# One recurrence head's projections and one more gate computed in the dense stage, read back from DRAM, and the first dense unit opened earlier

## The chip, the cores and the metric

The kernel runs on one core of a Trainium2 chip. The metric is the device time of the whole program in microseconds, the median of three runs. The engines have the names of the profile: PE (TensorE, matmuls and transposes), DVE (VectorE), ACT (ScalarE), POOL (GpSimd) and SP (SyncE, which here only issues DMAs). Each engine works off a list of instructions of its own in a fixed order.

## What is computed

One block of a streaming encoder over 1024 tokens of width 1024, in float32:

```python
h = rmsnorm(x, norm_mix_g)
z = h @ w_in          # hq hf hi hg | fq fk fv ff | mq | gate_logits
y_a = hgrn2(hq, hf, hi, hg)      # 4 heads, state 128 x 128
y_b = fox(fq, fk, fv, ff)        # 8 heads of 64, causal, forgetting
y_c = memory_attention(mq, mem)  # 4 heads of 128 over 256 tokens
gates = sigmoid(gate_logits).reshape(B, T, 3, 1024)
merged = gates[0]*(y_a @ w_br_hgrn) + gates[1]*(y_b @ w_br_fox) + gates[2]*(y_c @ w_br_mem)
x = x + merged @ w_out
x = x + conv_glu_ffn(rmsnorm(x, norm_ffn_g))
```

For a recurrence (HGRN2) head, three of the projections go through a nonlinearity before the scan: q by silu, the forget logit by a sigmoid, whose logarithm is summed along the chunk, and the output gate by silu. The fourth, hi, gives the values.

## The kernel before

Each float32 product is done as three matmuls on operands split into a high and a low part (`mm3`, L160 to L162: high x high, low x high, high x low). A split is a cast on ACT (L166) and a subtraction on DVE (L174); the weights' parts are wh and wl, the normed input's uh and ul. A projection goes in chunks of 128 output columns, each in two halves of 512 tokens. `cm_chunk` takes a half in 8 steps of 128 rows, 24 matmuls of 512 columns; a half sits in one of three PSUM banks (pp) until it is evacuated.

The stages, in the program's order:

1. First two gates, the memory's keys and values (`mem_values`, `mem_keys`), and a gate that covers what lies between (`first_cover`, `cover`). `SEQ` writes down the order of these steps. `differences` makes the families T1 to T4, sums and differences of blocks of the input, with their splits.
2. The dense stage. `dense_unit` takes two chunks at once by a Strassen-Winograd scheme: seven products in place of eight, each 4 x 3 matmuls, on sums of weight blocks (s1 to s4) that DVE adds and that are split like weights. `PAIRS` lists the chunks: the memory's queries (12 to 15), then gates. `put` adds what a product has to be added to, applies tanh to a gate and writes it to DRAM (`gd`; the queries to `mqd`).
3. The forgetting attention, four pairs of heads (`fox_attn(p, i)`), in which transposes, casts, softmax and the products po alternate between the engines. So that PE does not wait for them, matmuls that depend on nothing are woven in (`weave`): the next pair's projections, plain gate chunks (`gates_early`, their count in `NFOX`) and, in the last pair, the recurrence's values (`hgrn_values`, evacuated by ACT into Vf at L1001; Vf's place is also read by the split of the last attention values, vhl). Before the attention is over, the static order already holds the recurrence's first projections.
4. The recurrence. `open_hgrn` loads the masks (hmf, cast to hm at L989) and rs. `hgrn_prep(h)` computes a head's three projections: evacuation with the token's scale on DVE into gt or zt (L1032), tanh on ACT (L1034), then a clip and scale on POOL (ha, L1037) or a product on DVE (hq, hz, L1040). `hgrn_mix(h)` takes the head's logarithm (Ln, L1065), scans it (L1071), and does for each half a stack of levels with exponentials (Xk, X, L1081 to L1117), products pl (L1088), kE and its transposes (L1151 to L1160), states and po. Mix h is woven with the projections of head h + 1; head 0's run before the first mix.
5. Branches, output projection, and the feed-forward part.

[...] Where no other order is given, a scheduler sets each engine's list when the program is built; `ahead(..., AHEAD)` gives the woven attention and mixes priority, and `tc.issue_after` keeps an instruction behind a named other one. Buffers rotate within a tag (`bufs=`): the three gate tiles (gt) and the three banks pp matter here. `spread_dma` copies the norm's row to SBUF (L353) and sends it through DRAM to all partitions (rx), by which all gates are scaled.

Of the kernel before, what the change touches and what calls it, by code (L numbers as in the profile page):

```python
# [14 lines left out]
P = 128  # L15
# [76 lines left out]
def run_all(gen):  # L92
    for _ in gen:
        pass
# [15 lines left out]
def tile_block(ctx: ExitStack, tc: tile.TileContext, xT, memT, x_rows, mem_rows, vec, fbias, mats, hmask, w_first, w_cm, w_hi, w_fqk, w_fv,  # L110
# [20 lines left out]
    def ps_tr():  # L131
        return pz.tile([P, HB], F32, tag="tr", name="tr", bufs=2)
# [217 lines left out]
    def spread_dma(r, rcol, row, name, ps):  # L350

        PE.transpose(ps[:8, :P], rcol, ident)
        S.copy(row, ps[:8, :P])  # L353
# [50 lines left out]
    def mem_keys():  # L404
        mkt = keys[0]
        for hh in range(2):
            ptr = ps_tr()
            for h in range(2):
                for m in range(2):
                    PE.transpose(ptr[:, (2 * h + m) * P:(2 * h + m + 1) * P],  # L410
                                 mkt[:, m, (2 * hh + h) * P:(2 * hh + h + 1) * P], ident)
            S.activation(mkf[:, 2 * hh:2 * hh + 2, :], ptr.rearrange("p (h m) -> p h m", h=2), AF.Copy, scale=mgk)
        G.dma_start(kvd[:, 0, :], mkf.rearrange("p a b -> p (a b)"))
# [36 lines left out]

    gd = tc.dram_tile([len(order), 2, P, HB], F32, name="gd")
    mqd = tc.dram_tile([4, P, T], F32, name="mqd")

    home = {"pool": p0}

# [49 lines left out]
    def differences():  # L505

        b = [[xk[k + 4 * c][:, n * HB:(n + 1) * HB] for c in range(2) for n in range(2)] for k in range(4)]
        new_family(pt, "T1", 2)
        for t in range(4, 8):
            with tc.issue_after(late["keys"].ins), tc.issue_after(late["square"].ins):  # L510
                S.activation(xk[t], xk[t], AF.Copy, scale=col(C_GX + t))
        for k, (b11, b12, b21, b22) in enumerate(b):
            with tc.issue_after(late["x_low"].ins):
                V.tensor_sub(b11, b11, b12)
            h, l = (t[k] for t in fam["T1"])
            with tc.issue_after(late["square"].ins):
                S.activation(h, b11, AF.Copy, scale=col(C_GX + k))
            V.scalar_tensor_tensor(out=l, in0=b11, scalar=col(C_GX + k), in1=h.bitcast(F32), op0=ALU.mult, op1=ALU.subtract)
        yield
        new_family(pt, "T2", 2)  # L520
        for k, (t1, b12, b21, b22) in enumerate(b):
            with tc.issue_after(late["x mean"].ins):
                V.scalar_tensor_tensor(out=t1, in0=t1, scalar=ngx[:, k:k + 1], in1=b22, op0=ALU.mult, op1=ALU.subtract)
            family_block("T2", k, t1)
        yield
        new_family(pt, "T3")
        for k, (t2, b12, b21, b22) in enumerate(b):
            with tc.issue_after(late["x mean"].ins):
# [12 lines left out]

    gen = {}

    def families_step():
        if "differences" not in gen:
            gen["differences"] = differences()
        next(gen["differences"])

    named = dict(f1=families_step, f2=families_step, f3=families_step, mn=mem_norm, me=keys_out, mk=mem_keys, mv=mem_values, xn=x_norm, lk=load_late, lx=lambda: load_rows(*T2[2:], *T1[2:]), ly=lambda: load_rows(*T2[:2]), lz=lambda: load_rows(*T2[2:]), ev=first_gates, cv=first_cover)
    for what in SEQ:  # L550
        if what in named:
            named[what]()
        else:
            steps[what[0]](int(what[1]))
    p0.release()

    ps1 = Rounded(tc, name="ps1", bufs=1, side="right", reuse_waits="tile")
    def block(b, k):
        if b in fam:
            return [t[k] for t in fam[b]]  # L560
# [10 lines left out]
    class Dense:  # L571
# [1 line left out]
        half = None  # L573

        def snap(self, ps):
            e = ps1.tile([P, HB], F32, tag="fe", name="fe", bufs=3)
# [6 lines left out]
        def sum_of(self, i, a, b):  # L583
            t = ps1.tile([P, HB], F32, tag=f"s{i}", name=f"s{i}")
            V.tensor_add(t, a, b)
            return t

        def operand(self, src):
# [6 lines left out]
            split(S, h, l, src)  # L595
            return h, l

    dense = Dense()

    def dense_unit(src, put, first, families):  # L600

        raw = []
        whole = None if first else dense.raw()
        for i in range(2):
            if first:
                t = wp.tile([P, 4 * 264], F32, tag="raw", name="raw", bufs=2)[:, :2 * HB]
                t = t.rearrange("p (a b) -> p a b", a=2)
            else:
                t = whole[:, 2 * i:2 * i + 2, :]
            G.dma_start(t, src[:, 2 * i:2 * i + 2, :])  # L610
            raw += [t[:, 0, :], t[:, 1, :]]
        a11, a21, a22, a12 = raw
        x, y = ps_proj(), ps_lg()
        o1 = dense.operand(a11)
        if first:
            o6 = dense.operand(a12)
        s1 = dense.sum_of(1, a21, a22)
        o2 = dense.operand(s1)
        s2 = dense.sum_of(2, s1, a11)
# [12 lines left out]
        s4 = dense.sum_of(4, s2, a12)  # L632
        product(y, dense.operand(s4), "B22", False)
        put(0, 1, y, e2)
        s3 = dense.sum_of(3, a11, a21)
        product(x, dense.operand(s3), "T3", False)
        put(1, 1, x, e5)
        if not first:
            z = ps_tr()
            product(z, dense.operand(a12), "B21", True)  # L640
            put(0, 0, z, e1)
        product(x, dense.operand(a22), "T4", False)
        put(1, 0, x, None)

    def dense_put(chunks):

        def put(c, n, ps, e):
            ch = chunks[c]
            sl = slice(n * HB, (n + 1) * HB)
            t = gate_tile()  # L650
            if ch < 16:
# [357 lines left out]
    def held(gen, lag):  # L1009

        while True:
# [5 lines left out]
                    return  # L1017
            yield

    def hgrn_prep(h):  # L1020
        ph = state["ph"]
        qt = ph.tile([P, T], F32, tag="hq", name=f"hq_{h}", bufs=2)
        at = ph.tile([P, T], F32, tag="ha", name=f"ha_{h}", bufs=2)
        for what, base, dst in ((0, 4, at), (1, 0, qt), (2, 8, None)):
# [3 lines left out]
            for n, ps in cm_chunk(w_cm[base + h], KC, uh, ul, h == 3 and what == 2):  # L1028
                sl = slice(n * HB, (n + 1) * HB)

                zt = ph.tile([P, HB], F32, tag="zt", name="zt") if h else gate_tile()
                V.tensor_mul(zt, ps, rx[:, sl])  # L1032
                d = dst[:, sl]
                S.activation(d, zt, AF.Tanh, scale=0.5)  # L1034
# [766 lines left out]
```

## Time and profile before

| | |
|---|---|
| median of three runs | 1702.52 us (1702.37 to 1704.14) |
| profiled execution, its own time | 1703.12 us |
| its span, first to last instruction | 1701.3 us |
| granted TensorE clock | 1.000 |
| busy: PE, DVE, ACT, POOL | 99%, 68%, 47%, 19% |
| opening of the dense stage | about 69 to 86 us |
| last po of the attention | 682.6 us |
| first transposes of kE in the recurrence | 700.3 us |

In the rows of a timeline stand the start, the duration, the engine, the line, the operation, the tiles written and read, and in brackets the idle time before it with what ended it. A row of waits has the total, the number and the longest. A row of windows has the stretch, then the busy time and count of PE, of its weight loads, DVE, ACT and POOL, the granted clock, the DMAs' share and GB/s. Matmuls overlap, so the duration of one is not its cost; the distance of two starts is. The profiled execution is 0.6 us above the median of the runs.

### The profile page before, as it was taken

The page shows a single profiled execution, that of the slowest core. Times are in us where ns is not written, and L with a number is a line of the kernel's source. Part 1 is how long each engine was busy: PE and PEld are TensorE (multiplying, and loading weights), DVE is VectorE, ACT ScalarE, POOL GpSimd, SP SyncE. Part 2 cuts the span into 40 slices and gives each one's busy share as a digit, 9 for nine tenths or more (in the row PEclk, how much of TensorE's full clock was granted, in tenths as well). Part 3 has the DMA queues.
Part 4 walks back from the last instruction along what each step waited for, and adds up shares of the span by engine and source line. Part 5 has one row for each costly group of instructions (what it writes and reads, how often), then busy time and mean ns, then how long its engine had stood idle before and what let it go on. Part 6 is the DMA issues. An engine that isn't in the chain of part 4 may idle for free.

```text
span 1701.3 us, 24306 instructions
## 1 busy us (share of the span) xinstructions
PE 1692.3 (99%) x8965; PEld 1452.3 (85%) x8965; DVE 1151.9 (68%) x2057; ACT 801.5 (47%) x1428; POOL 326.7 (19%) x420
## 2 busy tenths in 40 slices
PE   9999999999999999999999999999999999999999
PEld 7788899989898998888888888888888888888887
DVE  6956555665666655786856855987778888775664
ACT  6734455555464553776531334644434444433432
POOL 0200022543433331553310000311111111100000
PEclk9999999999999999999999999999999999999999
DMA  9433242221312111200346552566555444494782
GB/s 369 170 137 114 73 146 76 77 92 45 99 50 87 52 57 57 67 27 18 100 125 216 165 188 99 162 171 172 151 144 141 118 144 147 162 375 142 247 274 87
DMA packets 82774, 227.16 MB, mean 134 GB/s; under 512 B 9680, under 2 KB 12248, under 8 KB 82528
## 3 DMA queue, kind: packets, MB, share of 16 engines
q1 hardware_dynamic: 64464, 160.99, 27.4%
q0 software_dynamic: 18048, 64.50, 13.5%
q8 instruction: 70, 1.15, 0.3%
q14 instruction: 48, 0.39, 0.1%
q10 hardware_dynamic: 144, 0.13, 0.0%
HBM read 180.72 MB, written 67.93 MB: 146 GB/s over the span
## 4 chain that ended last, share of the span: by engine, by line
PE 98%; DVE 1%; DMA 0%; ACT 0%; issue 0%; SPq 0%; DVEq 0%
PE pp L162 21%; PE pp L160 21%; PE pp L161 21%; PE lg L160 4%; PE lg L162 4%; PE lg L161 4%; PE tr L160 3%; PE tr L162 3%; PE tr L161 3%; PE po L951 1%; PE lg L910 1%; PE lg L909 1%; PE po L950 1%; PE po L160 1%; PE po L161 1%; PE po L162 1%
## 5 line engine op out<-in xcount | busy, mean ns | idle before, releaser
L160 PE MATMUL pp<-uh,wh 128*128 128x512 f32 x412 | 163.1, 396 | 0.0
L161 PE MATMUL pp<-ul,wh 128*128 128x512 f32 x412 | 162.9, 395 | 0.0
L162 PE MATMUL pp<-uh,wl 128*128 128x512 f32 x412 | 162.4, 394 | 0.0
L161 PE MATMUL pp<-wl,uh 128*128 128x256 f32 (+1 forms) x512 | 146.2, 286 | 0.0
L162 PE MATMUL pp<-wh,ul 128*128 128x256 f32 (+1 forms) x512 | 146.0, 286 | 0.0
L160 PE MATMUL pp<-wh,uh 128*128 128x256 f32 (+1 forms) x512 | 145.6, 285 | 0.0
L166 ACT CAST wh<-s 128x512 fp32r<-128x512 f32 x113 | 68.2, 620 | 130.8 <-PE pp L161 66.4
L166 ACT CAST wh<-raw 128x1024 fp32r<-128x1024 f32 (+2 forms) x76 | 67.7, 890 | 100.3 <-PE pp L161 88.2
L166 ACT CAST wh<-rw 128x512 fp32r<-128x512 f32 x87 | 53.2, 619 | 107.6 <-PE pp L161 72.0
L160 PEld LDWEIGHTS pp<-wh,uh 128*128 128x128 f32 x512 | 97.3, 190 | 1.2
L161 PEld LDWEIGHTS pp<-wl,uh 128*128 128x128 f32 x512 | 97.4, 190 | 1.0
L162 PEld LDWEIGHTS pp<-wh,ul 128*128 128x128 f32 x512 | 97.4, 190 | 0.9
L1443 POOL DMA_DIRECT2D rw<-in_w_up x44 | 24.1, 555 | 372.8 <-DVE wl L1336 171.8
L166 ACT CAST dwh<-wr 128x1024 fp32r<-128x1024 f32 (+1 forms) x41 | 40.2, 980 | 115.0 <-PE tr L161 40.4
L162 PEld LDWEIGHTS pp<-uh,wl 128*128 128x128 f32 x412 | 77.5, 188 | 15.1
L174 DVE TENSOR_TENSOR wl<-raw,wh 128x1024 fp32r<-128x1024 f32 (+2 forms) x75 | 78.0, 1040 | 18.1 <-ACT wh L166 17.9
L160 PEld LDWEIGHTS pp<-uh,wh 128*128 128x128 f32 x412 | 77.5, 188 | 14.6
L161 PEld LDWEIGHTS pp<-ul,wh 128*128 128x128 f32 x412 | 77.5, 188 | 14.5
L174 DVE TENSOR_TENSOR dwl<-wr,dwh 128x1024 fp32r<-128x1024 f32 (+1 forms) x41 | 46.3, 1130 | 33.6 <-ACT dwh L166 32.5
L925 ACT ACTIVATE pt<-pt,st 128x128 f32<-128x128 f32 (+3 forms) x64 | 49.7, 777 | 40.1 <-DVE st L922 32.0
L927 POOL TENSOR_SCALAR pt<-pt,st 128x128 f32<-128x128 f32 (+3 forms) x64 | 50.7, 793 | 77.5 <-DVE st L926 62.4
L1336 DVE TENSOR_TENSOR wl<-rw,wh 128x512 fp32r<-128x512 f32 x69 | 47.7, 705 | 22.5 <-PE pp L162 18.1
(497 smaller groups left out, 5123.9 us busy)
## 6 DMA issues: line engine op xcount, KB each, us to landing
rw<-in_w_up POOLq DMA_DIRECT2D x44, 512.0 KB, 4.9
sd<-in_w_dn POOLq DMA_DIRECT2D x30, 512.0 KB, 6.2
br<-yd SPq DMA_DIRECT2D x30, 512.0 KB, 5.3
raw<-in_w_cm SPq DMA_DIRECT2D x24, 512.0 KB, 3.4
gd<-gt SPq DMA_DIRECT2D x48, 256.0 KB, 2.0
gt<-gd SPq DMA_DIRECT2D x48, 256.0 KB, 2.7
yd<-fc SPq DMA_DIRECT2D x44, 256.0 KB, 3.0
wr<-sd SPq DMA_DIRECT2D x20, 512.0 KB, 4.6
```

What stands on the lines that cost most here:

```text
L160: PE.matmul(ps, lh, rh, start=first, stop=False, skip_group_check=more)
L161: PE.matmul(ps, lh, rl, start=False, stop=False, skip_group_check=more)
L162: return PE.matmul(ps, ll, rh, start=False, stop=last, skip_group_check=more)
L166: return S.copy(out, in_)
L174: return (sub or V).tensor_sub(l, src, h.bitcast(F32))
L909: PE.matmul(ps[:, :w], qa[i][:, tsl], kh[i][:, s0:s0 + w], start=True, stop=False)
L910: fox_sets[p][3] = PE.matmul(ps[:, :w], qa[i][:, tsl], kl[i][:, s0:s0 + w], start=False, stop=True)
L925: S.activation(pt[:, :ns], pt[:, :ns], AF.Exp, bias=st[:, 2:3], accum_out=st[:, 3:4])
L927: G.tensor_scalar(pt[:, :ns], pt[:, :ns], st[:, 3:4], 0.0, ALU.mult, ALU.add)
L950: PE.matmul(o, vhl[:, sb, :], ph[:, src], start=(sb == 0), stop=False)
L1336: late["split"] = V.tensor_sub(l, src, h.bitcast(F32))
L1443: late["raw"] = G.dma_start(raw[:, 2 * i:2 * i + 2, :], src[:, 2 * i:2 * i + 2, :])
```

## The change

Three projections of recurrence head 0 (chunks 4, 0 and 8) go into the dense stage, and one more gate with them: nine dense units in place of seven. `put` does what `hgrn_prep(0)` did (tanh, clip and scale, or the product) and writes the result to DRAM (`hd`, six writes of 256 KB); `hgrn_load` reads it back in three transfers of 512 KB in place of `run_all(hgrn_prep(0))`. The last pair of the attention loses its gate chunk (`NFOX[6]`). In `SEQ` the first dense unit is opened (`du`: loads, first sums and splits, which use spare places in xk) before the first gates' evacuation and the memory's keys; the casts of T1 and T3 are kept behind the copy of the norm's row on ACT; the keys' transposes use another PSUM bank. Head 1's projections now use the gate tiles.

```diff
-NCOVER, NPAIR = 2, 10
+NCOVER, NPAIR = 2, 11
-NFOX = [0, 3, 0, 3, 0, 3, 1]
+NFOX = [0, 3, 0, 3, 0, 3, 0]
+HEAD0 = {4: 0, 0: 1, 8: 2}
-_dense = [12, 13, 14, 15] + [16 + 8 * br + j for br, j in ORDER[4:4 + NPAIR]]
+_dense = [12, 13, 14, 15] + list(HEAD0) + [16 + 8 * br + j for br, j in ORDER[4:4 + NPAIR]]
...
-       "q0 me k4 q1 k5 c0 ly c1 lz q2 q3 k6 q4 q5 k7 d0 q6 q7 xn d1 mv f1 cv f2 ev mk f3").split()
+       "q0 me k4 q1 k5 c0 ly c1 lz q2 q3 k6 q4 q5 k7 d0 q6 q7 xn d1 mv cv f1 f2 f3 du ev mk").split()
...
-        S.copy(row, ps[:8, :P])
+        late["row"] = S.copy(row, ps[:8, :P])
...
-            ptr = ps_tr()
+            ptr = pkv[1][1]
...
-            with tc.issue_after(late["square"].ins):
+            with tc.issue_after(late["row"].ins):
                 S.activation(h, b11, AF.Copy, scale=col(C_GX + k))
...
-            family_block("T3", k, b12)
+            with tc.issue_after(late["row"].ins):
+                family_block("T3", k, b12)
...
+        def open(self, src, places=None):
+            ...
+            o1 = self.operand(a11)
+            o6 = self.operand(a12) if places else None
+            s1 = self.sum_of(1, a21, a22, places and places[0])
+            o2 = self.operand(s1)
+            s2 = self.sum_of(2, s1, a11, places and places[1])
+            return raw, o1, o6, o2, s2, self.operand(s2) if places else None
...
+    def first_unit():
+        with tc.issue_after(late["row"].ins):
+            gen["unit"] = dense.open(w_pair[0], (xk[4][:, HB:], xk[5][:, HB:]))
...
-        product(x, dense.operand(s2), "T2", False)
+        product(x, o3 or dense.operand(s2), "T2", False)
         e2 = dense.snap(x)
+        o4 = dense.operand(dense.sum_of(4, s2, a12, xk[6][:, HB:] if first else None))
...
+            if ch in HEAD0:
+                z = e if e is not None else home["sums"].tile([P, HB], F32, tag="fe", name="fe", bufs=3)
+                if e is not None:
+                    V.tensor_add(z, ps, e)
+                src = ps if e is None else z
+                if c:
+                    V.scalar_tensor_tensor(out=z, in0=src, scalar=-1.0, in1=rx[:, sl], op0=ALU.mult, op1=ALU.mult)
+                else:
+                    V.tensor_mul(z, src, rx[:, sl])
+                S.activation(t, z, AF.Tanh, scale=0.5)
+                if HEAD0[ch] == 0:
+                    V.tensor_scalar(t, t, TMIN, c1[:, 0:1], ALU.max, ALU.mult)
+                else:
+                    V.scalar_tensor_tensor(out=t, in0=t, scalar=1.0, in1=z, op0=ALU.add, op1=ALU.mult)
+                SP.dma_start(hd[HEAD0[ch]][:, sl], t)
+                return
...
+    small_consts()
     families = gen["differences"]
...
     weave((chain(fox_values(), fox_proj(0)), 25), (ahead(memory(), AHEAD), 4 * MEM_STEPS))
-    small_consts()
...
+    def hgrn_load():
+        ph = state["ph"]
+        at, qt, gz = (ph.tile([P, T], F32, tag=tag, name=f"{tag}_0", bufs=2) for tag in ("ha", "hq", "hz"))
+        for i, t in enumerate((at, qt, gz)):
+            SP.dma_start(t, hd[i])
+        hset[0] = (qt, at, gz)
...
-                zt = ph.tile([P, HB], F32, tag="zt", name="zt") if h else gate_tile()
+                zt = ph.tile([P, HB], F32, tag="zt", name="zt") if h > 1 else gate_tile()
...
-    run_all(hgrn_prep(0))
+    hgrn_load()
```

The diff does not show how the scheduler's lists change. In a row of an order stand the line, the operation, the tiles written and read, and the size. Lines of the changed kernel are some 35 higher: L1032 is L1067 there, L1065 is L1100, L1081 is L1116.

The first place is DVE at the end of the attention. yp is the last attention output's evacuation, hm the masks, gt a projection's half. Before, two gts follow yp:

```order
L955 TENSOR_TENSOR yp<-po,yp 64x256
L1032 TENSOR_TENSOR gt<-pp,rx 128x512 x2
L989 CAST hm_7328<-hmf 128x256
L989 CAST hm_7329<-hmf 128x256
L989 CAST hm_7330<-hmf 128x512
L1040 SCALAR_TENSOR_TENSOR hq_7346<-hq_7346,gt 128x512
```

In the changed kernel the masks' casts stand between:

```order
L984 TENSOR_TENSOR yp<-po,yp 64x256
L1017 CAST hm_7555<-hmf 128x256
L1017 CAST hm_7556<-hmf 128x256
L1017 CAST hm_7557<-hmf 128x512
L1067 TENSOR_TENSOR gt<-pp,rx 128x512 x2
L1075 SCALAR_TENSOR_TENSOR hq_7598<-hq_7598,gt 128x512 x2
```

The casts have moved ahead of two evacuations, which are head 1's now.

The second place is ACT at the start of the first mix, from kE's exponentials on. Before, the level's exponentials (Xk, X) follow at once:

```order
L1151 ACTIVATE kE<-Gt 128x128 x4
L1154 ACTIVATE eg<-Gt 128x4
L1156 ACTIVATE qe<-Gt 128x512
L1103 ACTIVATE nr<-Gt 128x4
L1154 ACTIVATE eg<-Gt 128x4
L1081 ACTIVATE Xk<-X 128x512
L1105 ACTIVATE X<-Gt 128x64
```

In the changed kernel the next head's Ln (L, from head 1's ha) and two loads of tables stand there:

```order
L1186 ACTIVATE kE<-Gt 128x128 x4
L1189 ACTIVATE eg<-Gt 128x4
L1191 ACTIVATE qe<-Gt 128x512
L1138 ACTIVATE nr<-Gt 128x4
L1100 ACT_TABLE_LOAD
L1100 ACTIVATE L<-ha_7599,c_188 128x1024
L1189 ACT_TABLE_LOAD
L1189 ACTIVATE eg<-Gt 128x4
L1116 ACTIVATE Xk<-X 128x512
```

Three rows have moved ahead of Xk; before, they stand some fifteen rows behind it.

The third place is PE in the attention of head (3,0), where the gate chunk was. po and tr are the attention's, lg its logits, pp with 256 columns the recurrence's values. Before:

```order
L951 MATMUL po<-pl,vhl 128x256
L950 MATMUL po<-ph,vhl 128x128
L951 MATMUL po<-pl,vhl 128x128
L909 MATMUL lg<-kh_3_5754,qa_3_5756 128x128
L938 MATMUL tr<-ident,pt 128x128
L910 MATMUL lg<-kl_3_5758,qa_3_5756 128x128
L160 MATMUL pp<-wh,uh_79 128x256
L161 MATMUL pp<-wl,uh_79 128x256
L162 MATMUL pp<-wh,ul_80 128x256
L160 MATMUL pp<-wh,uh_81 128x256
```

In the changed kernel, the same attention rows:

```order
L980 MATMUL po<-pl,vhl 128x256
L979 MATMUL po<-ph,vhl 128x128
L980 MATMUL po<-pl,vhl 128x128
L938 MATMUL lg<-kh_3_6045,qa_3_6047 128x128
L939 MATMUL lg<-kl_3_6049,qa_3_6047 128x128
L938 MATMUL lg<-kh_3_6045,qa_3_6047 128x512
L939 MATMUL lg<-kl_3_6049,qa_3_6047 128x512
L967 MATMUL tr<-ident,pt 128x128
L938 MATMUL lg<-kh_3_6045,qa_3_6047 128x256
L939 MATMUL lg<-kl_3_6049,qa_3_6047 128x256
```

The value matmuls have moved behind these rows.

More of the change, by code (lines that the diff above doesn't have):

```diff
@@ L452, in tile_block @@
     mqd = tc.dram_tile([4, P, T], F32, name="mqd")
+    hd = tc.dram_tile([3, P, T], F32, name="hd")
     home = {"pool": p0}
@@ L540, in differences @@
         yield
[L542 to L557, printed above, removed]
     def block(b, k):
@@ L575, in snap @@
         def snap(self, ps):
-            e = ps1.tile([P, HB], F32, tag="fe", name="fe", bufs=3)
+            e = home["sums"].tile([P, HB], F32, tag="fe", name="fe", bufs=3)
             S.copy(e, ps)
@@ L581, in raw, with sum_of @@
             return home["raw"].tile([P, 4, HB], F32, tag="rw", name="rw", bufs=2)
-        def sum_of(self, i, a, b):
-            t = ps1.tile([P, HB], F32, tag=f"s{i}", name=f"s{i}")
+        def sum_of(self, i, a, b, t=None):
+            t = t if t is not None else home["sums"].tile([P, HB], F32, tag=f"s{i}", name=f"s{i}")
             V.tensor_add(t, a, b)
@@ L596, in operand @@
             return h, l
-    dense = Dense()
-    def dense_unit(src, put, first, families):
[L602 to L611, printed above, removed]
+        def open(self, src, places=None):
+            raw = []
+            whole = None if places else self.raw()
+            for i in range(2):
+                if places:
+                    t = wp.tile([P, 4 * 264], F32, tag="raw", name="raw", bufs=2)[:, :2 * HB]
+                    t = t.rearrange("p (a b) -> p a b", a=2)
+                else:
+                    t = whole[:, 2 * i:2 * i + 2, :]
+                G.dma_start(t, src[:, 2 * i:2 * i + 2, :])
+                raw += [t[:, 0, :], t[:, 1, :]]
+            a11, a21, a22, a12 = raw
+            o1 = self.operand(a11)
[4 more added lines that the diff above has]
+            return raw, o1, o6, o2, s2, self.operand(s2) if places else None
@@ new lines, in tile_block, with families_step @@
+    dense = Dense()
+    gen = {}
+    def families_step():
+        if "differences" not in gen:
+            gen["differences"] = differences()
+        next(gen["differences"])
+    def first_unit():
+        with tc.issue_after(late["row"].ins):
+            gen["unit"] = dense.open(w_pair[0], (xk[4][:, HB:], xk[5][:, HB:]))
+    named = dict(du=first_unit, f1=families_step, f2=families_step, f3=families_step, mn=mem_norm, me=keys_out, mk=mem_keys, mv=mem_values, xn=x_norm, lk=load_late, lx=lambda: load_rows(*T2[2:], *T1[2:]), ly=lambda: load_rows(*T2[:2]), lz=lambda: load_rows(*T2[2:]), ev=first_gates, cv=first_cover)
@@ L612, in dense_unit @@
+    for what in SEQ:
+        if what in named:
+            named[what]()
+        else:
+            steps[what[0]](int(what[1]))
+    p0.release()
+    ps1 = home["sums"] = Rounded(tc, name="ps1", bufs=1, side="right", reuse_waits="tile")
+    def dense_unit(src, put, first, families):
+        raw, o1, o6, o2, s2, o3 = gen["unit"] if first else dense.open(src)
         a11, a21, a22, a12 = raw
         x, y = ps_proj(), ps_lg()
-        o1 = dense.operand(a11)
-        if first:
-            o6 = dense.operand(a12)
@@ L617, in dense_unit @@
-        s1 = dense.sum_of(1, a21, a22)
-        o2 = dense.operand(s1)
-        s2 = dense.sum_of(2, s1, a11)
         product(x, o1, "B11", True)
@@ L628, in dense_unit @@
         e5 = dense.snap(y)
-        product(x, dense.operand(s2), "T2", False)
+        product(x, o3 or dense.operand(s2), "T2", False)
         e2 = dense.snap(x)
+        o4 = dense.operand(dense.sum_of(4, s2, a12, xk[6][:, HB:] if first else None))
         run_all(families)
-        s4 = dense.sum_of(4, s2, a12)
-        product(y, dense.operand(s4), "B22", False)
+        product(y, o4, "B22", False)
         put(0, 1, y, e2)
@@ L650, in put @@
             t = gate_tile()
+            if ch in HEAD0:
[5 more added lines that the diff above has]
+                    V.scalar_tensor_tensor(out=z, in0=src, scalar=-1.0, in1=rx[:, sl], op0=ALU.mult, op1=ALU.mult)
+                else:
+                    V.tensor_mul(z, src, rx[:, sl])
+                S.activation(t, z, AF.Tanh, scale=0.5)
+                if HEAD0[ch] == 0:
+                    V.tensor_scalar(t, t, TMIN, c1[:, 0:1], ALU.max, ALU.mult)
+                else:
+                    V.scalar_tensor_tensor(out=t, in0=t, scalar=1.0, in1=z, op0=ALU.add, op1=ALU.mult)
+                SP.dma_start(hd[HEAD0[ch]][:, sl], t)
+                return
             if ch < 16:
```

## The prediction

> **What bounds the kernel now.** I read the page's totals first, then the chain of waits, then the waits of TensorE.
>
> ```profile
> span 1701.3 us, 24306 instructions
> PE 1692.3 (99%) x8965; PEld 1452.3 (85%) x8965; DVE 1151.9 (68%) x2057; ACT 801.5 (47%) x1428; POOL 326.7 (19%) x420
> PE 98%; DVE 1%; DMA 0%; ACT 0%; issue 0%; SPq 0%; DVEq 0%
> PE pp L160 <- ACT wh L166: 1.1, 1, 1.1
> PE tr L160 <- ACT mkf L412: 0.8, 1, 0.8
> PE pp L162 <- DVE wl L174: 0.5, 1, 0.5
> ```
>
> TensorE (PE) is the bound, and nearly without a gap. So two things change the time: how many matmuls PE has, and new waits of PE. A row removed from another engine gains nothing; a row that comes later on another engine costs only what PE waits for it. All of PE's waits together are 1701.3 - 1692.3 = 9.0 us, so no cure of waits can bring more.
>
> **The matmuls that go.** The pitch of PE is read from two starts of the same kind of instruction, in a stretch that holds only the 512-column matmuls of a projection:
>
> ```profile
> 683.01 0.39 PE L162 MATMUL pp<-uh,wl 128*128 128x512 f32 x1
> 700.04 0.39 PE L162 MATMUL pp<-uh,wl 128*128 128x512 f32 x1
> ```
>
> Three matmuls (L160, L161, L162) belong to each step, and 25 steps lie between these two: 17.03 / 75 = 0.227 us. (The 0.39 us of a row is its latency; matmuls overlap.) A plain chunk of 128 columns is 2 halves x 8 x 3 = 48 matmuls. A dense unit does two chunks with 7 products x 4 x 3 = 84, where two plain chunks are 96. Three projections of head 0 and one gate, 192 matmuls, become two units of 168: 24 fewer, **-5.4 us**. The two units' extra work on DVE and ScalarE (ACT) has room, as DVE is busy 53 of 100 us there, and the six writes of 256 KB too (DMA share 0.28):
>
> ```profile
> 100.00:200.00 100.00, 100.00 (x443) 82.81 (x442) 53.22 (x84) 39.58 (x71) 4.27 (x8) 1.00 0.28 97
> ```
>
> If that cover were gone, each of 12 halves (six of head 0) would cost one more DVE row of some 0.7 us; I take nothing.
>
> **The opening of the dense stage.** Three waits of PE lie here:
>
> ```profile
> 69.67 0.50 PE L160 MATMUL tr<-uh,wh 128*128 128x512 f32 x1 [0.78 <-ACT mkf L412]
> 84.68 0.50 PE L160 MATMUL pp<-T2h,wh 128*128 128x512 f32 x1 [1.05 <-ACT wh L166]
> 85.90 0.50 PE L162 MATMUL pp<-T2h,wl 128*128 128x512 f32 x1 [0.48 <-DVE wl L174]
> 60.70 0.25 ACT L353 COPY line<-pp 8x128 f32<-8x128 f32 x1
> ```
>
> The first waits for a bank that the memory keys' copy holds; with the keys' transposes in another bank it goes. The other two wait for the operand of T2, split only after B11 began; the opening done ahead has it ready. The copy of the norm's row, at 60.70 behind T1's and T3's casts, now comes ahead of them; the casts move back by 0.25 us and the DMA's way is shortened. 0.78 + 1.05 + 0.48 = **-2.3 us**. The sums and splits moved forward stand in DVE's row ahead of the first gates' evacuation; if those come late, this gain is given back, so its range is -2.3 to 0.
>
> **A hole in the last pair's attention.** Head (3,0) loses its gate chunk, 48 matmuls of cover. In the order of after, PE's rows from a transpose to the next head's last po hold none of the 48 value matmuls that stand among them before, because these lack a bank until Vf is evacuated, and that waits for the split of vhl:
>
> ```profile
> 605.40 0.27 PE L938 MATMUL tr<-ident,pt 128*128 128x128 f32 x1
> 616.18 0.28 PE L951 MATMUL po<-pl,vhl 128*128 128x128 f32 x1
> 606.28 0.42 DVE L915 CUSTOM_DVE_ANT_0 pt<-lg,nf 128x256 f32<-128x256 f32 x1 [0.76 <-PE tr L938]
> 609.92 0.16 DVE L926 RECIPROCAL st<-st 128x1 f32<-128x1 f32 x1 [0.94 <-ACT pt L925]
> 611.49 0.69 DVE L915 CUSTOM_DVE_ANT_0 pt<-lg,nf 128x512 f32<-128x512 f32 x1 [1.40 <-PE tr L938]
> 613.29 0.68 DVE L174 TENSOR_TENSOR vhl<-Vf,vhl 128x512 fp32r<-128x512 f32 x1
> 614.41 0.84 ACT L1001 ACTIVATE Vf<-pp,rt 128x256 f32<-128x256 f32 x2
> 600.00:620.00 20.00, 20.00 (x163) 19.64 (x162) 13.76 (x45) 11.87 (x26) 6.71 (x12) 1.00 0.20 64
> ```
>
> These rows took 616.30 - 605.40 = 10.9 us; 48 fillers at 20.0 / 163 = 0.12 us are 5.8 of it, so PE's own part is 5.1. The serial part is: 0.9 us to DVE's row at 606.28; from there to the end of vhl at 613.97 7.7 us, less the two idle times 0.94 and 1.40, 5.4; one evacuation, 0.84 / 2 = 0.4. Together 6.7, so PE waits **+1.6 us**; as DVE also waits for ACT and POOL once or twice, I take **+2**, between 0.5 and 3.
>
> **From attention to recurrence.** Before, the 77 matmuls that follow the last po (the rest of head 0's, then head 1's) find free banks. After, head 1's six halves are the fillers of the attention, all done by the last po, three of them still in the three banks. The next matmul, head 2's first, needs a bank, so the evacuation (gt, L1032 before, L1067 after) of the fourth half on DVE. There three casts of the masks (hm) now stand ahead of that gt, and they wait for a DMA that SP issues behind the last ybd:
>
> ```profile
> 682.61 0.28 PE L951 MATMUL po<-pl,vhl 128*128 128x128 f32 x1
> 682.73 0.45 PE L161 MATMUL pp<-ul,wh 128*128 128x512 f32 x1
> 682.93 0.37 ACT L954 COPY yp<-po 64x256 f32<-64x256 f32 x1 [5.65 <-PE po L951]
> 683.77 0.45 SPq L956 DMA_DIRECT2D ybd<-yp  x1
> 684.27 0.58 SPq L986 DMA_DIRECT2D hmf<-in_hmask  x1
> 683.87 1.29 DVE L1032 TENSOR_TENSOR gt<-pp,rx 128x512 f32<-128x512 f32 x2
> 686.73 0.83 DVE L989 CAST hm<-hmf 128x256 uint8<-128x256 f32 x3 [1.58 <-DMA hmf<-in_hmask]
> ```
>
> By these rows gt ends at 686.73 + 0.75 + 0.65 = 688.1 rather than 684.5, and PE, which would have gone on at 682.73, stands 5.4 us. What it meets next decides the sum: L1123 (pl of level 0, L1088 before), 56 matmuls and four transposes on. Unhindered, PE is there at 682.73 + 56 x 0.227 + 0.35 = 695.8. Its operand X is the end of ACT's chain:
>
> ```profile
> 691.19 1.28 ACT L1065 ACT_TABLE_LOAD   x1
> 692.48 1.15 ACT L1065 ACTIVATE L<-ha,c 128x1024 f32<-128x1024 f32 x1
> 695.59 1.26 ACT L1151 ACTIVATE kE<-Gt 128x128 f32<-128x128 f32 x4
> 697.58 0.62 ACT L1081 ACTIVATE Xk<-X 128x512 f32<-128x512 f32 x1
> 701.82 0.68 DVE L1084 TENSOR_TENSOR X<-X,hq 128x512 f32<-128x512 f32 x1
> 704.13 1.28 ACT L1065 ACT_TABLE_LOAD   x1
> br<-yd SPq DMA_DIRECT2D x30, 512.0 KB, 5.3
> raw<-in_w_cm SPq DMA_DIRECT2D x24, 512.0 KB, 3.4
> ```
>
> In after's order Ln of head 0 stands behind hq and hz (which need the gts) and behind the first of three hd reads. The reads are issued at about 685.4, behind hmf and rs; 3.4 to 5.3 us to landing by the nearest rows give 688.8 to 690.7. The gts give 688.1 + 2 x 0.65 = 689.4. I take 690.0. Then table 1.28, Ln 1.15, table 1.28, hz 0.6, nr and kE 1.3, eg, qe and nr 0.8: 696.4. There a second pair of tables with head 1's Ln, which before came after these exps (704.13), now stands ahead of them: 1.28 + 1.15 + 1.28 + 0.1 = 3.8, 700.2. From Xk to the end of L1084 it was 702.50 - 697.58 = 4.9: X at 705.1. So PE loses 705.1 - 695.8 = **+9.3 us** here in all, the 5.4 included. The bounds: reads landing at 688.8 and all at its shortest, 7.5; reads at 690.7, 10. I take **+9**.
>
> On the tables, the row of Ln starts at 692.48, right behind its table load. [...]
>
> **The recurrence's mixes.** From kE's transposes to the last po PE had 841 rows and has 725, as head 1's matmuls are spent earlier: 26.3 us less cover over the same DVE chain.
>
> ```profile
> 700.00:880.00 180.00, 179.99 (x1065) 153.65 (x1065) 135.13 (x227) 108.35 (x266) 65.81 (x58) 1.00 0.19 58
> ```
>
> DVE had 135 us of work in 180; less head 1's ten rows or so (some 9 us) it has 126 in 154. That is 82%, not a bound on the mean, but between some of the o2 transposes there are 23 DVE rows of about 0.6 us (14 us) against 72 PE rows (15 us). I take **+2**, from 0 to 6.
>
> **The sum.** -5.4 - 2.3 + 2 + 9 + 2 = +5.3 us on the profiled execution's 1703.1. The median of the runs, 1702.5, lies 0.6 lower, and I put the same difference on it: **1707.8 us**. What a measurement can tell from no change is 0.2%, 3.4 us: 1699.1 to 1705.9.
>
> **Rivals.**
>
> *Half covered* (about no change). The hd reads land at once and the hole and the mixes cost their least: -7.7 + 0.5 + 7.5 + 0 = +0.3, 1702.8. For it: the mean use of DVE; against it: the two places in DVE's and ACT's rows, which do not depend on the reads. Chance 0.23.
>
> *Faster: the masks land under the attention.* If the hmf, rs and hd transfers are through before the last po, PE waits only for ACT's yp copy, a tanh and the gt: to about 684.5, 1.8 us, and X's chain starts 4 to 5 us earlier with head 1's Ln waiting for its own inputs. Then -7.7 + 0.5 + 3 + 0 = -4.2, 1698.3; it is faster from the point where the three added terms stay below 4.3 us. Against it: in the trace hmf is issued at 684.27, after the last yp, and SP's row has it there still. Chance 0.12.
>
> *DVE sets the mixes' pace.* If the 126 us of DVE meet in each group of levels what PE has, PE waits 1 to 2 us in each of the seven halves after the first: +8 in place of +2, 1713.8. The 18.3 us of 20 that DVE reached at its fullest would speak for it:
>
> ```profile
> 820.00:840.00 20.00, 20.00 (x106) 16.77 (x105) 18.28 (x29) 12.46 (x32) 5.62 (x5) 1.00 0.24 73
> ```
>
> Chance 0.13.
>
> *PE comes back slowly.* After a wait of 5.4 and one of some 4 us the matmuls behind could come at twice their pitch for a while. In this trace PE never stands longer than 1.1 us and the granted clock is 1.00 in each window, so no row bears it out. Eight matmuls late by 0.227 each are +1.8, 1709.6. [...] Chance 0.14.
>
> The forecast itself: 0.38, by its bounds 1703.5 to 1711. Faster: 0.12. Within 0.2%: the half-covered case and a little of the forecast, 0.27. Slower: the rest, 0.61. The range must hold 8 in 10; it runs from the faster case's edge to the mixes' case, 1699.5 to 1714.
>
> **What would show it.** Right: 5784 in place of 5808 matmuls of 512 columns; no wait for mkf, and none for T2; a wait of PE for gt (L1067) of about 5.4 us and one at L1123 of about 4; hm's casts waiting for hmf; Ln of head 1 ahead of Xk; a wait in the (3,0) attention of 1 to 3. Wrong: PE's waits at the transition below 4 in sum, or more than 5 us of waits in the mixes.

## The result and the profile after

The changed kernel is slower: a median of 1724.78 us (1724.20 to 1727.62) beside 1703.26 us (1702.37 to 1704.14) for the kernel before, a ratio of 1.0130 with a 95% interval of 1.0112 to 1.0147. The forecast had the sign, 1707.8 us, but the time lies far outside its range of 1699.5 to 1714.

The page's totals of the changed kernel (its profiled execution took 1727.62 us, the mean granted clock was 0.992):

```profile
span 1725.8 us, 24330 instructions
PE 1700.0 (99%) x8941; PEld 1458.0 (84%) x8941; DVE 1162.9 (67%) x2083; ACT 809.2 (47%) x1444; POOL 323.8 (19%) x422
```

The profiled execution is the slowest of the four, 2.8 us above their median: the spans differ by 24.5 us, the medians by 21.5. PE's idle time (span less busy) went from 9.0 to 25.8, 16.8 more. PE's busy time went from 1692.3 to 1700.0, 7.7 more, with 24 matmuls fewer, which are worth 5.4: so the matmuls that are left took 13.1 us longer. The mean clock says the same: 0.008 of 1725.8 us is 13.8.

PE's waits, with total, count and longest:

```profile
PE pp L161 <- DVE gt L1067: 6.9, 1, 6.9
PE tr L1239 <- ACT o L1232: 3.4, 1, 3.4
PE lg L1123 <- DVE X L1119: 2.5, 2, 1.8
PE po L1210 <- DVE St L1216: 2.2, 2, 1.4
PE po L1210 <- DVE St L1214: 1.7, 2, 1.3
PE lg L938 <- DVE st L944: 0.6, 2, 0.3
```

The waits for mkf and for T2 are gone. Of the waits shown, all but the last (in the attention of head (3,0)) lie between the last po at 712.48 us and the end of the mixes.

The transition in time (start, duration, engine, line, idle time before):

```profile
712.48 0.27 PE L980 MATMUL po<-pl,vhl 128*128 128x128 f32 x1
714.93 0.54 SPq L1014 DMA_DIRECT2D hmf<-in_hmask  x1
716.01 0.42 SPq L1052 DMA_DIRECT2D ha<-hd  x1
718.13 0.83 DVE L1017 CAST hm<-hmf 128x256 uint8<-128x256 f32 x3 [3.83 <-DMA hmf<-in_hmask]
719.61 0.80 PE L161 MATMUL pp<-uh,wh 128*128 128x512 f32 x1 [6.86 <-DVE gt L1067]
720.21 0.63 PE L162 MATMUL pp<-ul,wh 128*128 128x512 f32 x1
720.63 0.63 PE L163 MATMUL pp<-uh,wl 128*128 128x512 f32 x1
722.09 1.28 ACT L1100 ACT_TABLE_LOAD   x1 [1.26 <-DMA ha<-hd]
729.76 1.15 ACT L1100 ACTIVATE L<-ha,c 128x1024 f32<-128x1024 f32 x1
737.33 1.13 PE L1123 MATMUL lg<-X,Xk 128*128 128x128 f32 x8 [1.83 <-DVE X L1119]
```

This is the stretch that the prediction described, in its order: the masks' casts wait for their transfer, gt stands behind them, PE stands, and Ln of head 1 (729.76), with a table load of 1.28 us ahead of it and one behind (728.47 and 730.92), delays X. New are the distances of the matmuls behind the wait: 0.42 us from 720.21 to 720.63 in place of 0.227. The windows show why (the column behind POOL is the granted clock):

```profile
708.00:712.00 4.00, 4.00 (x21) 3.33 (x20) 0.44 (x1) 0.33 (x1) 0.00 (x0) 1.00 0.00 0
720.00:724.00 4.00, 4.00 (x10) 3.09 (x10) 2.56 (x5) 2.72 (x4) 1.61 (x2) 0.50 0.96 352
796.00:800.00 4.00, 4.00 (x22) 3.66 (x22) 2.98 (x6) 2.79 (x9) 2.08 (x3) 0.50 0.13 47
860.00:864.00 4.00, 4.00 (x13) 3.32 (x14) 2.64 (x5) 1.46 (x5) 1.97 (x2) 0.50 0.00 0
```

The second and third low stretches follow the waits in the mixes: L1239 (3.38 us, ending at 794.00) and L1210 with L1175 (1.26, 1.41 and 0.38 us, ending at 859.12). A smaller one, 0.80 in 736 to 740 and 0.77 in 740 to 744, follows L1123 (1.83 us).

### The profile page after: what moved, and what is told of

Its sections match the earlier page's. It is cut to its first block, busy times and chain, and to the rows that moved or that the text cites. A ratio compares the mean times of both kernels' runs of the same rounds, so it can differ in the third digit from the quotient of the medians.

```text
span 1725.8 us, 24330 instructions
## 1 busy us (share of the span) xinstructions
PE 1700.0 (99%) x8941; PEld 1458.0 (84%) x8941; DVE 1162.9 (67%) x2083; ACT 809.2 (47%) x1444; POOL 323.8 (19%) x422
## 4 chain that ended last, share of the span: by engine, by line
PE 95%; DVE 2%; ACT 2%; DMA 1%; issue 1%; SPq 0%; POOL 0%; DVEq 0%; POOLq 0%; ACTq 0%
PE pp L161 20%; PE pp L163 20%; PE pp L162 20%; PE lg L161 5%; PE lg L162 4%; PE lg L163 4%; PE tr L163 3%; PE tr L161 3%; PE tr L162 3%; PE po L980 1%; PE lg L939 1%; PE lg L938 1%; PE po L979 1%; PE po L161 1%; PE po L162 1%; PE po L163 1%
## 5 line engine op out<-in xcount | busy, mean ns | idle before, releaser
L161 PE MATMUL pp<-uh,wh 128*128 128x512 f32 x356 | 142.3, 400 | 6.9 <-DVE gt L1067 6.9
L163 PE MATMUL pp<-uh,wl 128*128 128x512 f32 x356 | 141.7, 398 | 0.0
L162 PE MATMUL pp<-ul,wh 128*128 128x512 f32 x356 | 141.2, 397 | 0.0
L167 ACT CAST wh<-rw 128x512 fp32r<-128x512 f32 x93 | 56.7, 619 | 117.0 <-PE pp L162 79.4
L167 ACT CAST wh<-raw 128x1024 fp32r<-128x1024 f32 (+2 forms) x72 | 63.4, 882 | 93.3 <-PE pp L162 79.5
L1478 POOL DMA_DIRECT2D rw<-in_w_up x44 | 24.1, 554 | 376.5 <-DVE wl L1371 181.7
L175 DVE TENSOR_TENSOR wl<-raw,wh 128x1024 fp32r<-128x1024 f32 (+2 forms) x71 | 72.4, 1020 | 24.1 <-ACT wh L167 24.0
L161 PEld LDWEIGHTS pp<-uh,wh 128*128 128x128 f32 x356 | 67.9, 191 | 19.9 <-DVE gt L1067 7.0
L163 PEld LDWEIGHTS pp<-uh,wl 128*128 128x128 f32 x356 | 67.7, 190 | 13.4
L162 PEld LDWEIGHTS pp<-ul,wh 128*128 128x128 f32 x356 | 67.7, 190 | 12.8
L1371 DVE TENSOR_TENSOR wl<-rw,wh 128x512 fp32r<-128x512 f32 x69 | 46.5, 688 | 21.5 <-PE pp L163 18.2
```

The lines of the kernel that those rows point to most:

```text
L161: PE.matmul(ps, lh, rh, start=first, stop=False, skip_group_check=more)
L162: PE.matmul(ps, lh, rl, start=False, stop=False, skip_group_check=more)
L163: return PE.matmul(ps, ll, rh, start=False, stop=last, skip_group_check=more)
L167: return S.copy(out, in_)
L175: return (sub or V).tensor_sub(l, src, h.bitcast(F32))
L1371: late["split"] = V.tensor_sub(l, src, h.bitcast(F32))
```

## The experiments

The theory after the result: the waits come from two causes, the order of the lists at the transition and the cover that the mixes lost, and the waits cost the clock as well (0.50 in 720 to 724 us, behind the 6.86 us). Rivals: the order alone is the cause and the mixes' waits are its echo; or the clock fell for a reason of its own. Ratios are to the kernel before, with 95% intervals.

**The opening alone.** Head 0 and the gates as before, the rest of the change kept:

```diff
-NCOVER, NPAIR = 2, 11
+NCOVER, NPAIR = 2, 10
-NFOX = [0, 3, 0, 3, 0, 3, 0]
+NFOX = [0, 3, 0, 3, 0, 3, 1]
-HEAD0 = {4: 0, 0: 1, 8: 2}
+HEAD0 = {}
...
-    hgrn_load()
+    run_all(hgrn_prep(0))
```

> The changed kernel's opening of the dense stage alone: head 0's projections and the gates are where they were before. If the three waits of the opening (0.78, 1.05 and 0.48 us) go and nothing comes in their place, it is 2.3 us faster than the kernel before. Rival: they are only moved, and it is within 0.5 us of before. Neither theory expects a granted clock below 1.00.

1699.58 us beside 1702.97, ratio 0.9978 (0.9968 to 0.9987): 3.4 us faster, and the fastest whole kernel of this study. PE's busy time and waits:

```profile
PE 1691.0 (100%) x8965; PEld 1452.4 (86%) x8965; DVE 1150.2 (68%) x2057; ACT 801.3 (47%) x1428; POOL 326.8 (19%) x420
PE po L1210 <- DVE St L1216: 0.7, 1, 0.7
```

The dense stage's opening has no wait left; the idle time is 1697.9 - 1691.0 = 6.9 us, 2.1 less than before. PE's busy time is 1.3 us lower too, with as many matmuls; no wait explains that part. So all of the changed kernel's loss, and more, comes from head 0 and the gates: 1724.78 - 1699.58 = 25.2 us.

**Head 1's Ln later.** Held behind the first mix's exponentials (x0 and x1 are those of its levels 32 and 0):

```diff
-        S.activation(Lt, at, AF.Ln, bias=c0[:, h:h + 1])
+        with tc.issue_after(state["x0"].ins) if h == 1 else nullcontext(), tc.issue_after(state["x1"].ins) if h == 1 else nullcontext():
+            S.activation(Lt, at, AF.Ln, bias=c0[:, h:h + 1])
```

> The changed kernel with head 1's Ln (and its two table loads) held behind the first mix's exponentials. If that order is what makes PE wait at L1123, the wait of 1.8 us there goes and with it the low clock behind it (0.80 and 0.77 in 736 to 744): 2 to 4 us less than the changed kernel, with the wait of 6.9 for gt as it was. Rival: the low clock has a cause of its own, and stays where it was.

1720.74 us, 1.0099 (1.0084 to 1.0114): 4 us less than the changed kernel, as expected. The wait at L1123 is gone, and the granted clock in 736 to 744 us is 1.00 in place of 0.80 and 0.77. But new waits stand behind it:

```profile
736.54 1.16 PE L1203 MATMUL tr<-Vf,kT 128*128 128x128 f32 x8 [1.44 <-ACT kT L1200]
791.21 0.65 PE L1166 MATMUL lg<-X 128*64 128x64 f32 x8 [2.82 <-DVE X L1156]
```

**The whole order at the transition.** The masks' casts behind the evacuation of head 1's fourth half, the hd reads first in SP's row, and Ln later as above:

```diff
+        hgrn_load()
         state["rs"] = ph.tile([P, HB], F32, tag="rs", name="rs")
...
+    first = hgrn_prep(1)
+    for _ in range(4):
+        next(first)
+    with tc.issue_after(state["gt"].ins):
+        state["masks"]()
```

> The changed kernel with the masks' casts behind the evacuations of head 1, the hd reads ahead of the masks' transfer, and head 1's Ln behind the first exponentials. Theory: waits from the attention to the first mix fall from 8.7 us to 2 or 3, and no wait there is long enough for the clock, so some 9 us less than the changed kernel; the mixes' waits (8 us together, and two stretches of low clock) stay, as they come from the cover that was taken away. Rival: the mixes' waits are an echo of the late start, and go too: 18 us less.

1729.75 us, 1.0153 (1.0137 to 1.0168), 5 us slower than the changed kernel; both theories were wrong on this run. The wait for gt shrank to 2.2 us (the clock behind it still fell, to 0.50 in 716 to 718 us) and the one for X is gone, but PE now waits for kE and kT a little later, and longer in the mixes (L1169, L1216):

```profile
PE lg L1169 <- DVE X L1159: 5.3, 1, 5.3
PE po L1216 <- DVE St L1220: 2.9, 1, 2.9
PE tr L1201 <- DVE kE L1193: 2.6, 2, 2.3
PE pp L161 <- DVE gt L1070: 2.2, 1, 2.2
PE tr L1206 <- ACT kT L1203: 2.0, 2, 1.7
```

The first transposes of kE started at these times:

```profile
700.27 0.60 PE L1160 MATMUL tr<-ident,kE 128*128 128x128 f32 x4
730.10 0.60 PE L1195 MATMUL tr<-ident,kE 128*128 128x128 f32 x4
729.35 1.09 PE L1201 MATMUL tr<-ident,kE 128*128 128x128 f32 x4 [2.25 <-DVE kE L1193]
```

(Before, changed kernel, this one.) From the start of the last po that is 17.66, 17.62 and 17.51 us, with 77, 35 and 48 matmuls of projections between, and 0, 6.9 and 4.5 us of PE's waiting. That these times are so near each other is partly chance: kE was ready (the end of its row on DVE) 15.7, 16.3 and 17.4 us after the last po, so in the first two PE came 2.0 and 1.3 us after it, and in the third PE waited for it. The way from the last po through the masks or reads, the gts, Ln, the scan and kE takes its time; 77 matmuls (17.5 us) cover it, 35 (7.9 us) or 48 (10.9 us) do not. So the wait at the transition too is missing cover; this order moved the waits and did not shorten the way.

**A wait by itself.** The kernel before, with PE made to wait in its dense stage for a chain on POOL (the edit of the second try):

```diff
+        if len(units) in (2, 4, 6):
+            G.tensor_scalar(idle[:, :8], late["t"][:, :8], 0.0, 1.0, ALU.mult, ALU.add)
+            for _ in range(len(units) // 2 - 1):
+                G.tensor_tensor(idle[:, :8], idle[:, :8], mhalf[:, :8], ALU.pow)
+            for ps in (x, y):
+                PE.matmul(ps[:8, :8], idle[:, :8], idle[:, :8], start=True, stop=True)
```

A first try tied the chain to no result of PE:

> The kernel before, with PE made to wait three times in the middle of its dense stage for one, two and four small operations of POOL (some 2, 4 and 8 us). Nothing else is changed; the wait is added work. If the clock follows the wait, it is 1.00 after the shortest and falls to 0.5 for some microseconds after the longer ones, so that 512-column matmuls come at 0.43 in place of 0.23 us, 2 to 3 us lost each time beside the wait. Rival: the clock in the changed kernel fell for another reason, and it stays 1.00 here after each wait.

POOL ran it ahead of time and PE did not wait for it: 1705.06 us in one run, clock 1.000, nothing learned. With the chain behind the unit's last evacuation:

> The kernel before, with PE made to wait three times in its dense stage, at the starts of the third, fifth and seventh unit, for a chain that begins with the last evacuation and ends with one, two and three small operations of POOL: waits of some 2, 4 and 6 us, which are added work. If the clock follows the wait, it is 1.00 behind the first and falls to 0.5 for some microseconds behind the second and the third, and 512-column matmuls start 0.43 us apart there: 2 to 3 us lost each time beside the wait. Rival: the clock of the changed kernel fell for another reason, and stays 1.00 here.

1719.03 us, also one run. The scheduler spread the waits over the unit's end, so they are shorter than meant (0.8 to 1.4 us each, and one of 0.2). They still tell the two apart. Three rows of PE ahead of the fifth unit, and two windows:

```profile
157.93 0.50 PE L160 MATMUL tr<-uh,wh 128*128 128x512 f32 x1 [1.06 <-ACT wh L166]
159.86 0.80 PE L162 MATMUL tr<-uh,wl 128*128 128x512 f32 x1 [1.20 <-DVE wl L174]
160.45 0.63 PE L160 MATMUL tr<-uh,wh 128*128 128x512 f32 x1
160.00:162.00 2.00, 2.00 (x5) 1.63 (x6) 0.41 (x1) 0.00 (x0) 1.92 (x2) 0.50 0.30 115
206.00:208.00 2.00, 1.30 (x9) 1.10 (x10) 0.00 (x0) 0.00 (x0) 0.64 (x1) 1.00 0.03 8
```

Behind two waits, 1.06 and 1.20 us, the second 1.9 us after the first, the clock was halved (0.50 in 160 to 162 us), in a stage and a kernel that have nothing of the change. Behind one of 1.35 us at 206.69, 3.9 us behind the wait before it, it was not (1.00, the second window). So the clock fell behind PE's own idling, without anything of the change, but not behind every wait.

**Cover given back.** The changed kernel with two gates out of the dense stage and into the first two mixes, 12 matmuls more:

```diff
-NCOVER, NPAIR = 2, 11
+NCOVER, NPAIR = 2, 9
...
-        weave((ahead(hgrn_mix(h, ya), AHEAD), HGRN_STEPS), (hgrn_prep(h + 1), 6))
+        weave((ahead(hgrn_mix(h, ya), AHEAD), HGRN_STEPS), (hgrn_prep(h + 1), 6), (gates_early(int(h < 2)), 2))
```

> The changed kernel with two gates taken out of the dense stage and woven into the first two mixes: head 0 still comes from the dense stage and through DRAM, PE has 12 matmuls of 512 columns more than the changed kernel (2.7 us), and the mixes have 96 more that wait for nothing. If the lost cover is the cause, the mixes' waits (8 us) and the low clock behind them (some 6 us) go for the most part: 1712 to 1716. Rival: the transition's order alone is the cause; then it is 2 to 3 us slower than the changed kernel.

1708.30 us, 1.0032 (1.0022 to 1.0042): 16.5 us less than the changed kernel, though PE has more to do, and 3.7 us below what was expected. The transition gained too: its code was not touched, but the scheduler put 69 fillers ahead of kE where the changed kernel has 35, and the wait for gt shrank:

```profile
PE 1693.0 (99%) x8953; PEld 1451.5 (85%) x8953; DVE 1153.1 (68%) x2071; ACT 805.0 (47%) x1436; POOL 329.8 (19%) x420
PE pp L161 <- DVE gt L1067: 2.7, 1, 2.7
```

This run is still 8.7 us slower than the opening alone. No run separates what of that is the way of head 0 through DRAM.

**Cover and order.** The two gates in the mixes, the masks' casts and Ln later, and the hd reads where the change has them:

```diff
+        weave((ahead(hgrn_mix(h, ya), AHEAD), HGRN_STEPS), (hgrn_prep(h + 1) if h else first, 6 if h else 2), (gates_early(int(h < 2)), 2))
```

> The changed kernel with both: two gates woven into the first two mixes, the masks' casts behind the evacuations, and head 1's Ln behind the first exponentials. If order and cover together are the whole cause, the waits of transition and mixes fall to 3 us and the clock stays at 1.00: the opening's 3.4 and 12 matmuls fewer than before (2.7) leave it at 1697 to 1700. Rival: DVE and ACT set the pace of the mixes, whatever the cover; then it stays above 1710.

1711.90 us, 1.0050 (1.0035 to 1.0065): neither theory's number. The rival's bound holds, but not its mechanism: behind the transition PE idles 0.2 us in 156 us of the mixes (the window below). With cover, the repaired order is 3.6 us slower than without the repair. The scheduler put 39 fillers ahead of kE here, where it had 69 in the run before, so PE reached kE 11.1 us after the last po and waited there for 3.5 us:

```profile
PE tr L1200 <- DVE kE L1192: 3.8, 2, 3.5
PE tr L1205 <- ACT kT L1202: 2.8, 2, 2.5
724.00:880.00 156.00, 155.83 (x923) 131.98 (x922) 115.20 (x197) 92.07 (x235) 56.59 (x51) 1.00 0.19 65
```

**Cover taken from the kernel before.** The projections of heads 1 to 3 leave out the first two of their eight steps:

```diff
-            for k in range(nk):
+            for k in range(left_out, nk):
...
+            for n, ps in cm_chunk(..., left_out=2 * min(h, 1)):
```

> The kernel before, with the first two of eight steps of the projections of heads 1 to 3 left out (those sums are incomplete): 96 matmuls fewer, 21.8 us of PE's work, all from the cover of the mixes; the transition, the dense stage and head 0 are untouched. If the mixes need that cover, PE waits instead, more than 8 us, with a low clock behind, and the kernel gains less than 12 us of the 21.8. Rival: the mixes have slack enough, and it gains 20 to 22 us.

1697.10 us, 0.9962 (0.9947 to 0.9977): 21.8 us of matmuls less, and 6.0 us gained. PE idles 1695.9 - 1676.2 = 19.7 us in place of 9.0, and the mean clock is 0.996:

```profile
span 1695.9 us, 24115 instructions
PE 1676.2 (99%) x8869; PEld 1437.9 (85%) x8869; DVE 1149.0 (68%) x2057; ACT 800.5 (47%) x1428; POOL 327.2 (19%) x420
PE lg L1128 <- DVE X L1118: 2.2, 1, 2.2
PE lg L1140 <- DVE X L1118: 2.0, 1, 2.0
```

The transition keeps its cover here (79 fillers, no wait of PE). Of the 21.8 us, 10.7 came back as waits, and PE's busy time fell by 16.1 only, so 5.7 came back as slower matmuls. The mixes of the kernel before can spare at most some 11 us of cover before PE waits, and taking 21.8 gains 6.

**Cover in another place.** As with cover given back, but the two gates are woven into the attention of head (3,0):

```diff
-NCOVER, NPAIR = 2, 11
+NCOVER, NPAIR = 2, 9
-NFOX = [0, 3, 0, 3, 0, 3, 0]
+NFOX = [0, 3, 0, 3, 0, 3, 2]
```

> As the run with two gates returned to the mixes, with the same matmuls, but the two gates are woven into the last pair's attention (3,0) instead. If it matters that the cover lies in the mixes, this one stays near the changed kernel: its mixes have as few matmuls that wait for nothing, 2.7 us are added and at most 1 us of waits in the attention goes, 1722 to 1728. Rival: any cover from the attention on will do, as head 1's projections then stay for the mixes; then 1708, as there.

1717.09 us, 1.0084 (1.0069 to 1.0099): between the two theories' numbers, 7.7 us less than the changed kernel and 8.8 us more than with the same gates in the mixes. The transition has 83 fillers and PE waits for nothing there until X (0.9 us), though head 0's reads lie there as in the changed kernel; then the mixes run short, at one place above all:

```profile
PE lg L1163 <- DVE X L1153: 6.2, 1, 6.2
```

**More dense units from the attention.** The opening alone with one more unit, its two gates from the attention of pairs one and three, then (second `NFOX`) of pairs two and three:

```diff
-NCOVER, NPAIR = 2, 10
+NCOVER, NPAIR = 2, 12
-NFOX = [0, 3, 0, 3, 0, 3, 1]
+NFOX = [0, 2, 0, 3, 0, 2, 1]
...
+NFOX = [0, 3, 0, 2, 0, 2, 1]
```

> The opening alone, with one more dense unit whose two gates come from the attention of the first and the third pair, where PE never waits in the profile of before; head 0 stays where it was before. 12 matmuls fewer: 2.7 us less than the opening alone if the attention has that cover to spare, 1696.5 to 1697.5. Rival: the attention needs the cover as the mixes do, PE waits there, the clock follows, and it is 5 us or more slower than the opening alone.

> As the run before it, with the two gates taken from the second and the third pair's attention. The same 2.7 us if the attention has cover to spare in every pair; if only some pairs have, this one and the run before it differ by the waits of one pair.

1718.98 us (1.0095, 1.0078 to 1.0111) and 1713.10 us (1.0058), 12 matmuls fewer and 19 and 14 us slower than the opening alone. The attention has no cover to spare either, and both runs also wait at the transition, which is left with 48 and 52 fillers though head 0 is where it was. Only a part of that was drawn into the attention: behind the last po 432 matmuls of the recurrence's projections are left in both runs, where the opening alone has 446, so the rest of the difference is their order. The first run's longest waits:

```profile
PE tr L1195 <- DVE kE L1187: 2.9, 1, 2.9
PE pp L161 <- DVE gt L1067: 2.2, 1, 2.2
PE pp L161 <- ACT z L867: 2.0, 1, 2.0
```

## Why the prediction was right or wrong

- **The matmuls (-5.4).** Right: 8941 PE instructions in place of 8965.
- **The opening (-2.3).** Right: the three waits are gone, 2.3 us; by itself the opening measured -3.4, of which 2.1 is waiting.
- **The hole in (3,0) (+2).** Too dear: 0.25 and 0.33 us at L938. The cover was missing in the order, but the chain was not shorter than I added it up: the stretch without value matmuls, 635.94 to 644.01, took 8.1 us where I had 6.7. PE's own rows filled 7.1 us of it in place of 5.1, so PE idled 1.0.
- **The transition (+9).** Its mechanism and place were right, and so was the size of the waits, 8.7 us, though not their parts: 6.86 for gt in place of 5.4 and 1.83 at L1123 in place of about 4, as some 2.5 us of low clock behind the first wait had used up part of the second. With that low clock PE reached L1123 at 737.33, 11.7 us later than 712.6 + 13.1. The bound on the transfers was too low: from hd's issue at 716.01 to the release of ACT at 722.09 it took 6.1 us (bounds 3.4 to 5.3), and hmf 3.2 where before it had been 2.5, issued 0.8 us later behind the last po. What the prediction did not see is that the order was not the whole cause: 42 of the 77 fillers were gone, and the two other orders that were tried gave back at most 13 of them.
- **The mixes (+2, up to 6).** This step failed first: 8.2 us of waits against 0.7 before, so +7.5, beyond its range and beyond the 5 us that the prediction itself named as a sign of being wrong. I compared DVE's mean load (82%) and one short segment. The load does not tell the three kernels below apart: from kE's transposes to the last po of the mixes DVE is busy 74%, 72% and 73% of the time, and PE idles 0.8, 10.1 (with the 1.83 at L1123) and 3.9 us. What differs is PE's work there, 1092, 975 and 1035 matmuls. What needs covering is the serial way through ACT, DVE and POOL from level to level; this is read from the rows that ended the waits (o on ACT, St and X on DVE), and no run isolates it.

```profile
700.27:884.96 184.69, 183.93 (x1092) 157.16 (x1091) 137.55 (x232) 109.16 (x267) 65.54 (x57) 1.00 0.19 59
730.10:907.90 177.80, 167.74 (x975) 143.76 (x974) 127.86 (x221) 104.60 (x268) 67.01 (x57) 0.94 0.16 53
711.78:889.30 177.52, 173.62 (x1035) 147.22 (x1034) 128.73 (x226) 106.57 (x272) 70.75 (x57) 0.99 0.21 66
```

  (The kernel before, the changed kernel, and the one with cover given back.) The rival that DVE sets the mixes' pace had the size nearly right (+8), but by luck: it put 1 to 2 us into each of seven halves, and 6.4 of the 8.2 us lie at two places, around 794 and 857 us, the longest behind ACT.
- **PE comes back slowly (a rival at 0.14, +1.8).** This step failed most: 13.1 us, over half of the loss. The sum had nothing for it, and the rival priced eight matmuls behind one wait; the eight were an estimate of mine that no run shows. Measured, the clock stayed low for microseconds behind four groups of waits, at 720, 736 to 744, 796 and 860; they follow waits of 6.86, of 1.83, of 3.38 and of 1.26 + 1.41 us. Behind the first alone the 12 matmuls from 719.61 to 724.85 took 5.24 us, where 12 x 0.227 are 2.7.
- **The sum.** -5.4 and -2.3 as forecast; +8.7 at the transition, +7.5 in the mixes, some +2.5 of small waits from the start to the feed-forward part, +13.1 of clock: +24.1 of the 24.5 by which the profiled spans differ.

Shown by runs: the cover's worth (returned twice, taken once, displaced once), the clock's link to waits, the opening's gain. Argued only: the serial way as what needs cover, and why the repaired order is slower than the one it replaces; the traces show its waits at other places, not why their sum grew.

## What to carry to other kernels

On an engine that is 99% busy, matmuls that wait for nothing are what hides the other engines' chains. They are a budget, and it matters where they lie: taking 96 of them away from the mixes (21.8 us) gained only 6, the same two gates gave 16.5 us back in the mixes and 7.7 in the attention, and moving four chunks to a cheaper place saved 5.4 us of work and cost some 30 (25.2 more than the opening alone, and the 5.4 that it saved). Before filler work is made cheaper or moved, the question is what each of its matmuls covers; a mean load of the other engines does not answer it, the serial way from one wait to the next does. And a wait that the order of a list explains can come back at the next row when the order is changed: here less waiting for gt and X became waiting for kE and kT.

## What the runs showed of the hardware

The clock's answer to waits was dearer and less regular than expected. Half the clock came after 6.86 us of idling, and after 1.06 and 1.20 us within 3 us. A single wait of 2.20 us brought it down in the run with the whole order at the transition; a wait of the same 2.20 us did not in the second run with more dense units, nor did one of 2.65 us in the run with cover given back, all in front of a projection's matmuls. A window behind each:

```profile
716.00:718.00 2.00, 2.00 (x6) 1.52 (x6) 0.66 (x2) 0.00 (x0) 1.93 (x1) 0.50 0.91 340
690.00:692.00 2.00, 2.00 (x10) 1.66 (x9) 0.23 (x1) 0.00 (x0) 1.91 (x3) 1.00 0.77 254
702.00:704.00 2.00, 2.00 (x10) 1.66 (x9) 1.29 (x3) 1.97 (x3) 1.84 (x2) 1.00 0.75 297
```

So the length of a single wait does not decide it here; what does, no run shows. After the 6.86 us PE's matmuls ran at the half clock from 719.6 to about 724.8 (0.50 in 720 to 724, 0.90 in 724 to 728).
